# A two-block fp32 network on one core: SyncE stores queued one step behind the work that makes them, and FFN operands made one block in advance

## The chip, the cores and the metric

One core of a Trainium2 chip runs the whole network in one program. The metric is the device time of one execution in microseconds (us). Lower is better.

## What is computed

Block 1 puts four mixers side by side (mLSTM, SGU, a convolution, S5), joins them through `w_out`, and then runs the part that the change touches:

```python
x = layer_norm(ALPHA * x + g1 * y, ln1_w[l], ln1_b[l])
x = layer_norm(ALPHA * x + g2 * swiglu(x * (1.0 + sc2) + sh2, w_ffn_in[l], w_ffn_out[l]), ln2_w[l], ln2_b[l])
# swiglu: g, u = split(h @ w_in); (silu(g) * u) @ w_out
```

x has 1024 tokens of 1024 features, and the hidden width is 2816; all of it is in fp32. Block 2 (retention, sparse attention, a gated embedding) follows and is left as it is.

## The kernel before

**Arithmetic.** Every large product is made of three fp32r products. `K.split` writes a high part on ScalarE (ACT, L173, or L176 with a scale) and the rest on VectorE (DVE, L174 or L177), and `K.gemm` issues three matmuls per pair (L184 to L186: high by high, high by low, low by high).

**FFN input.** The 2816 hidden columns go in 22 blocks j of 128 (gate and up together). Each block is a product of 2 by 2 blocks done with seven products instead of eight, of 12 matmuls of 128x512 each: `Ffn.one` (two gate products, operands "11" and "12"), `two` (s2 by t2, s1 by t1), `three` (s4 by 22, s3 by t3) and `four` (22 by t4), 84 matmuls per block. For the weights, `Ffn.load` fetches two raw pages of w_ffn_in (L409), GpSimd (POOL) makes four sums (fsa, fsb: L424, L425, L429, L430), and seven splits make the operands `fw`. The activations come from `low_half` (11, 21) and `high_half` (t1, t2, 22, t3, t4), once, in the head of this stage. `first` issues the gate products of blocks 0 and 1, and `rest` goes through the blocks with the gate products two blocks ahead.

**FFN output.** `stage_b` takes the hidden blocks in 8 groups of two or three. For each group, 8 token tiles of two halves each are multiplied (18 matmuls per tile where the group has three hidden blocks) and DVE adds the result into `acc` (L615). `load(blk)` brings the next group: activations from scratch memory through `wload` (L160), weights (L562) with a POOL product by g2 (L563), and splits of both.

**What else runs there.** `residual()` reads 8 tiles back (L542), scales them (DVE L543, POOL L544) and stores them (L545). `spare` is the generator `presplit`: it loads 28 tiles of block 2's w_in (L771) and 16 of two later weights (by `wload`), splits them and stores both parts (L777, L783). `Ffn.four` stores each hidden block to scratch (L484).

**What sets the order.** The generators are advanced by hand in `stage_b`; the tile framework then places each instruction on its engine's queue. All loads and stores stand in one queue, SyncE's (SP), and are issued in its order: an issue that waits holds all behind it. Fetched fp32 pages come from a ring of three raw pages (`rp`, NR = 3), everything else from 46 pages (`qp`). PSUM has two rings of four banks (`mm`, `ax`).

Of the kernel before, what the change touches and what calls it, by code (L numbers as in the profile page):

```python
# [21 lines left out]
DFF = 2816  # L22
# [94 lines left out]
class K:  # L117
    def __init__(self, tc, es):
        self.tc, self.nc = tc, tc.nc
        self.es = es  # L120
# [135 lines left out]
class Front:  # L256
# [101 lines left out]
    def high_half(self):  # L358

        k, nc, page, s1, t1, hf, B = self.k, self.k.nc, self.k.page, self.s1, self.t1, self.hf, self.B  # L360
        fs, sp = [], {}

        def split(n, i, x):
            if i % 2 == 0:
                sp[n] = [page(f"{n}{c}{i}", F32R, [128, 2, 512]) for c in "hl"]
            hi, lo = (x[:, i % 2] for x in sp[n])
            nc.scalar.activation(hi, x, AF.Copy)
            nc.vector.tensor_tensor(lo, x, hi, op=ALU.subtract)
            B[n].append((hi, lo))
# [19 lines left out]
        for i in range(4):  # L389
            yield 1  # L390
            nc.gpsimd.tensor_tensor(fs[i][:, 0], fs[i][:, 1], fs[i][:, 0], op=ALU.subtract)
            split('t3', i, fs[i][:, 0])
        hf.clear()


class Ffn:
# [1 line left out]


    def __init__(self, k, B, w_fi, act):  # L400
        self.k, self.B, self.w_fi, self.act, self.w, self.o, self.keep = k, B, w_fi, act, {}, {}, {}

    def load(self, j):

        k, nc = self.k, self.k.nc
        raw = []
        for i in range(2):
            r = k.raw([128, 8, 128])
            nc.sync.dma_start(r, dap(self.w_fi, (i * (DFF // 128) + j) * 131072, [[1024, 128], [128, 8], [1, 128]]))  # L409
            raw.append(r)  # L410
        (a11, a12), (a21, a22) = [(r[:, 0:4], r[:, 4:8]) for r in raw]
        self.w[j] = w = {}

        def split(n, x):
            p = k.wpage("fw", shape=[128, 2, 4, 128])
            k.split(p[:, 0], p[:, 1], x)
            w[n] = p[:, 0], p[:, 1]

        split('11', a11)
        split('12', a12)  # L420
        yield 1
# [4 lines left out]
        split('s1', sp[:, 0])  # L426
        split('s2', sp[:, 1])
        yield 1
        nc.gpsimd.tensor_tensor(sq[:, 0], a12, sp[:, 1], op=ALU.subtract)  # L429
        nc.gpsimd.tensor_tensor(sq[:, 1], a11, a21, op=ALU.subtract)  # L430
        split('s4', sq[:, 0])
        yield 1
        split('s3', sq[:, 1])
        split('22', a22)

    def prod(self, j, a, b, pool):
        k, nc = self.k, self.k.nc
        ps = pool.tile([128, 512], F32, name="mm" if pool is k.mm else "ax")
        a, B = self.w[j].pop(a), self.B[b]
# [14 lines left out]
    def two(self, j):  # L454

        k, nc = self.k, self.k.nc
        e, u = self.o[j] = self.o[j], k.page("fu", shape=[128, 2, 512])
        nc.vector.tensor_tensor(u[:, 0], self.prod(j, 's2', 't2', k.ax), e[:, 1], op=ALU.add)
        yield 1
        nc.vector.tensor_tensor(u[:, 1], self.prod(j, 's1', 't1', k.ax), u[:, 0], op=ALU.add)  # L460

    def three(self, j):

# [10 lines left out]
    def four(self, j):  # L474
# [10 lines left out]
        del self.w[j]  # L485

    def first(self):
        self.ld = [self.load(0), self.load(1), self.load(2)]
        next(self.ld[0])
        next(self.ld[1])  # L490
        yield 1
        while len(self.B['21']) < 4:
            yield 1
        for j in range(2):
            yield from self.one(j)
            yield 1
            for _ in self.ld[j]:
                pass

    def rest(self):  # L500
        n = DFF // 128
        ld = self.ld[2]
        for j in range(n):
            for _ in self.two(j):
                next(ld, None)
            yield j, 0
            if j:
                self.four(j - 1)
            next(ld, None)
            for _ in self.three(j):  # L510
                next(ld, None)
            for _ in ld:
                pass
            ld = self.load(j + 3) if j + 3 < n else iter(())
            next(ld, None)
            if j + 2 < n:
                for _ in self.one(j + 2):
                    pass
            yield j, 1
        self.four(n - 1)  # L520


KEPT = (19, 20, 21)
FBLOCKS = ((19, 20), (21, 0, 1), (2, 3, 4), (5, 6, 7), (8, 9, 10), (11, 12, 13), (14, 15, 16), (17, 18))

# [1 line left out]
def stage_b(k, front, mod_s, ln1_w, ln1_b, w_fo, ln2_w, ln2_b, x2_s, sink, early, pre_sink, after, background, spare):  # L527
# [5 lines left out]
    def residual():  # L533
# [6 lines left out]
        for t in range(8):  # L540
            r = page("resid")
            nc.sync.dma_start(r, dap(res, t * 131072, [[1024, 128], [1, 1024]]))  # L542
            nc.vector.tensor_tensor(r, r, aw, op=ALU.mult)  # L543
            nc.gpsimd.tensor_tensor(r, r, ab, op=ALU.add)  # L544
            nc.sync.dma_start(dap(res2, t * 131072, [[1024, 128], [1, 1024]]), r)  # L545
            yield 1

    def load(blk):

        A, W = [], []  # L550
        yield A, W
        for j in blk:
            if j in keep:
                e = keep.pop(j)
                hl = page("ah", F32R), page("al", F32R)
                k.split(*hl, e)
                A.append(hl)
            else:
                A.append(k.wload(dap(act, j * 131072, [[1024, 128], [1, 1024]]), [128, 1024]))
            yield 1  # L560
            raw = k.raw()
            nc.sync.dma_start(raw, dap(w_fo, j * 131072, [[1024, 128], [1, 1024]]))  # L562
            nc.gpsimd.tensor_tensor(raw, raw, g2[0], op=ALU.mult)  # L563
            hl = page("whi", F32R), page("wlo", F32R)
            k.split(*hl, raw)
            W.append(hl)
            yield 1

    rs = residual()
    ahead = load(FBLOCKS[0])  # L570
    for j, st in front.ffn.rest():
        if st == 0 and 2 <= j < 18:
            for _ in range(1 + j % 2):
                next(spare, None)
        if st == 1 and j >= 2:
# [4 lines left out]
        if (j, st) == (19, 1):  # L580
            for t in range(8):
                acc[t] = page(f"acc{t}")
                nc.sync.dma_start(acc[t], dap(res2, t * 131072, [[1024, 128], [1, 1024]]))
        if (j, st) == (21, 0):
            nxt = next(ahead)
            next(ahead)
            next(ahead)
    for n, blk in enumerate(FBLOCKS):
        last = n == len(FBLOCKS) - 1
        for _ in ahead:  # L590
# [2 lines left out]
        if n == 5:  # L593
            early()
        if last:
            for _ in spare:
                pass
# [35 lines left out]
        else:  # L633
            for t in range(8):
                for _ in next(items):
                    pass
                next(ahead, None)
                if t % 3 == 1:
                    next(spare, None)


# [61 lines left out]
class StageC:  # L703
# [61 lines left out]
    def presplit(self):  # L765

        k, nc, w = self.k, self.k.nc, self.I['w_in']
        for b, (c0, n) in enumerate(WBLOCKS):
            for kk in range(0, 8, 2):
                raw = k.raw([128, 2, n])  # L770
                nc.sync.dma_start(raw, dap(w, kk * 128 * 3512 + c0, [[3512, 128], [128 * 3512, 2], [1, n]]))  # L771
                hi = k.wpage("phi", shape=[128, 2, n])
# [3 lines left out]
                for i, x in enumerate((hi, lo)):  # L776
                    nc.sync.dma_start(self.wsplit_at(b, kk, i, n), x.rearrange("p a b -> p (a b)").bitcast(F32))  # L777
                yield None
        for m, (w, sc, n) in enumerate(self.late):
            for kk in range(8):  # L780
                hl = k.wload(dap(w, kk * 131072, [[1024, 128], [1, 1024]]), [128, 1024], sc[:, kk:kk + 1] if kk < n else None)
                for i, x in enumerate(hl):
                    nc.sync.dma_start(self.wlate_at(m, kk, i), x.bitcast(F32))  # L783
                yield None

    @property
# [1752 lines left out]
```

## Time and profile before

| | |
|---|---|
| median of 3 runs | 2141.87 us (2139.83 to 2141.97) |
| the profiled execution | 2143.97 us, span 2142.2 us |
| mean granted TensorE clock | 0.962 of full |
| PE busy | 1978.5 us, 92% |
| DVE, ACT, POOL busy | 67%, 40%, 26% |
| DMA | 157 GB/s over the span |

Times are read from the start of the span. The high half of the activations is made from 622 to 667 us, the FFN's input products run until about 1089, its output products until about 1342, and block 2 takes the rest. A wait "X <- Y" says that engine line X was idle until Y was done. A busy PE (TensorE) can still be slow: the granted clock says at which of its two levels it ran.

### The profile page before, as it was taken

The page shows a single profiled execution, that of the slowest core. Times are in us where ns is not written, and L with a number is a line of the kernel's source. Part 1 is how long each engine was busy: PE and PEld are TensorE (multiplying, and loading weights), DVE is VectorE, ACT ScalarE, POOL GpSimd, SP SyncE. Part 2 cuts the span into 40 slices and gives each one's busy share as a digit, 9 for nine tenths or more (in the row PEclk, how much of TensorE's full clock was granted, in tenths as well). Part 3 has the DMA queues.
Part 4 walks back from the last instruction along what each step waited for, and adds up shares of the span by engine and source line. Part 5 has one row for each costly group of instructions (what it writes and reads, how often), then busy time and mean ns, then how long its engine had stood idle before and what let it go on. Part 6 is the DMA issues. An engine that isn't in the chain of part 4 may idle for free. (4 is left out here: it accounts for less than half of the span.)

```text
span 2142.2 us, 29434 instructions
## 1 busy us (share of the span) xinstructions
PE 1978.5 (92%) x10544; PEld 1630.6 (76%) x10544; DVE 1426.6 (67%) x2832; ACT 848.7 (40%) x1696; POOL 558.2 (26%) x557
## 2 busy tenths in 40 slices
PE   8798898999987989999999889899999998899998
PEld 3797888877865877778887768786787786688886
DVE  6968636476788567767666584957788746856533
ACT  2521234342144333334323220545787625355432
POOL 1454403112144333432412210331011221200032
PEclk9999898989998999999999999999999998999999
DMA  8465464456612566655556764313412205343611
GB/s 290 157 161 145 137 196 149 166 174 213 221 49 68 174 214 235 228 209 205 213 176 237 253 235 162 138 40 105 151 50 89 88 26 162 129 153 119 226 60 69
DMA packets 154419, 336.05 MB, mean 157 GB/s; under 512 B 31768, under 2 KB 71192, under 8 KB 154272
## 3 DMA queue, kind: packets, MB, share of 16 engines
q1 hardware_dynamic: 154272, 334.16, 46.2%
q8 instruction: 83, 1.36, 0.3%
q14 instruction: 64, 0.52, 0.1%
HBM read 227.16 MB, written 105.91 MB: 155 GB/s over the span
## 5 line engine op out<-in xcount | busy, mean ns | idle before, releaser
L184 PE MATMUL mm<-whi,xTh 128*128 128x512 f32 (+1 forms) x576 | 229.0, 401 | 4.9 <-DMA whi<-scr_wsp 3.6
L185 PE MATMUL mm<-wlo,xTh 128*128 128x512 f32 (+1 forms) x576 | 226.1, 393 | 2.1 <-DMA wlo<-scr_wsp 2.1
L186 PE MATMUL mm<-whi,xTl 128*128 128x512 f32 (+1 forms) x576 | 224.9, 393 | 0.0
L184 PE MATMUL mm<-whi,hhi 128*128 128x256 f32 (+1 forms) x512 | 151.7, 296 | 1.6 <-ACT zd L1651 0.9
L186 PE MATMUL mm<-whi,hlo 128*128 128x256 f32 (+1 forms) x512 | 149.2, 292 | 1.9 <-POOL hlo L1553 1.5
L173 ACT ACTIVATE whi<-raw 128x1024 fp32r<-128x1024 f32 (+2 forms) x74 | 76.6, 1044 | 187.2 <-POOL raw L563 98.3
L185 PE MATMUL mm<-wlo,hhi 128*128 128x256 f32 (+1 forms) x512 | 150.0, 293 | 0.0
L174 DVE TENSOR_TENSOR wlo<-raw,whi 128x1024 fp32r<-128x1024 f32 (+2 forms) x74 | 95.0, 1284 | 75.9 <-ACT whi L173 75.8
L184 PE MATMUL ax<-whi 128*128 128x512 f32 x304 | 123.6, 406 | 17.4 <-DVE acc L615 17.3
L184 PEld LDWEIGHTS mm<-whi,xTh 128*128 128x128 f32 x576 | 109.5, 191 | 27.5 <-DMA whi<-scr_wsp 5.4
L185 PEld LDWEIGHTS mm<-wlo,xTh 128*128 128x128 f32 x576 | 109.9, 191 | 22.0 <-DMA wlo<-scr_wsp 2.9
L186 PEld LDWEIGHTS mm<-whi,xTl 128*128 128x128 f32 x576 | 109.8, 191 | 21.5 <-DVE xTl L849 0.8
L185 PE MATMUL ax<-wlo,whi 128*128 128x512 f32 x304 | 121.5, 400 | 0.7 <-DVE wlo L174 0.7
L186 PE MATMUL ax<-whi,wlo 128*128 128x512 f32 x304 | 121.3, 399 | 0.0
L952 ACT ACTIVATE junk<-score,candf 128x384 bf16<-128x384 f32 (+1 forms) x124 | 96.1, 775 | 34.2 <-DVE candf L973 31.6
L563 POOL TENSOR_TENSOR raw<-raw,g2b 128x1024 f32<-128x1024 f32 x22 | 55.9, 2542 | 196.3 <-DMA raw<-in_w_ffn_out 133.3
L184 PEld LDWEIGHTS mm<-whi,hhi 128*128 128x128 f32 x512 | 100.8, 197 | 3.8 <-ACT zd L1651 1.3
L186 PEld LDWEIGHTS mm<-whi,hlo 128*128 128x128 f32 x512 | 100.5, 197 | 3.2 <-POOL hlo L1553 1.9
L185 PEld LDWEIGHTS mm<-wlo,hhi 128*128 128x128 f32 x512 | 100.8, 197 | 0.8 <-issue 0.6
L615 DVE TENSOR_TENSOR acc<-ax,acc 128x512 f32<-128x512 f32 x128 | 84.3, 682 | 23.1 <-PE ax L186 23.1
L184 PEld LDWEIGHTS ax<-whi 128*128 128x128 f32 x304 | 59.0, 194 | 36.5 <-DVE acc L615 21.8
L184 PE MATMUL mm<-hh,fw 128*128 128x512 f32 x176 | 72.1, 410 | 14.6 <-ACT fw L173 14.6
(687 smaller groups left out, 5464.1 us busy)
## 6 DMA issues: line engine op xcount, KB each, us to landing
raw<-in_w_fi_o SPq DMA_DIRECT2D x44, 512.0 KB
wmr<-in_w_mod SPq DMA_DIRECT2D x32, 512.0 KB
raw<-in_w_in_2o SPq DMA_DIRECT2D x24, 512.0 KB
scr_wsp<-phi SPq DMA_DIRECT2D x24, 512.0 KB
scr_wsp<-plo SPq DMA_DIRECT2D x24, 512.0 KB
whi<-scr_wsp SPq DMA_DIRECT2D x24, 512.0 KB
wlo<-scr_wsp SPq DMA_DIRECT2D x24, 512.0 KB
raw<-in_w_ffn_out SPq DMA_DIRECT2D x22, 512.0 KB
```

Source lines behind the costliest of these rows:

```text
L173: nc.scalar.activation(hi, raw, AF.Copy)
L174: nc.vector.tensor_tensor(lo, raw, hi, op=ALU.subtract)
L184: nc.tensor.matmul(ps, ah, bh, start=k == 0, stop=False)
L185: nc.tensor.matmul(ps, ah, bl, start=False, stop=False)
L186: nc.tensor.matmul(ps, al, bh, start=False, stop=k == n - 1)
L563: nc.gpsimd.tensor_tensor(raw, raw, g2[0], op=ALU.mult)
L615: nc.vector.tensor_tensor(v[:, cs], ps, v[:, cs], op=ALU.add)
L952: nc.scalar.activation(junk[:, :w], x, AF.Sign, scale=-1.0, bias=c, accum_out=cnt[:, j:j + 1])
```

## The change

Stores: `put` remembers a store, `tick` issues what was remembered at the next step, behind that step's work. Splits of spare weights, residual tiles and FFN-out loads come one step after their load. `Ffn.load` is cut in three: `fetch` (the DMA), `gates` (two splits) and `sums` (POOL and five splits); `rest` makes gates and sums of block j+1 during block j, has four steps per block in place of two, and issues the gate products one block ahead, after the first three blocks' have been issued in `first`. The raw pages of the first blocks come from the 46 pages ("fr"). `high_half` makes t1 and t2, then 22, then t3, then t4 (before: t4 ahead of 22). `two` multiplies s1 by t1 first. Spare halves are advanced more often during FFN input (56 half steps, 28 items; before 24 items) and five halves per FFN-out group (before three whole items).

```diff
+    def put(self, *pairs):
+        self.puts += pairs
+    def tick(self):
+        for dst, src in self.puts:
+            self.nc.sync.dma_start(dst, src)
+        self.puts = []
...
         for i in range(4):
-            nc.gpsimd.tensor_tensor(hf[i + 4], hf[i + 4], hf[i], op=ALU.subtract)
-            split('t4', i, hf[i + 4])
-        for i in range(4):
             yield 1
             split('22', i, fs[i][:, 1])
...
+        for i in range(4):
+            nc.gpsimd.tensor_tensor(hf[i + 4], hf[i + 4], hf[i], op=ALU.subtract)
+        for i in range(4):
+            yield 1
+            split('t4', i, hf[i + 4])
...
-            nc.sync.dma_start(dap(self.act, j * 131072, [[1024, 128], [1, 1024]]), e)
+            k.put((dap(self.act, j * 131072, [[1024, 128], [1, 1024]]), e))
...
     def first(self):
+        for j in range(AHEAD):
+            self.fetch(j, 0, self.k.page)
+        self.fetch(0, 1, self.k.page)
         yield 1
+        self.gates(0)
+        self.gates(1)
         while len(self.B['21']) < 4:
             yield 1
+        sums = self.sums(0)
+        for j in range(AHEAD):
             yield from self.one(j)
+            if j + 2 < AHEAD:
+                self.gates(j + 2)
+            else:
+                next(sums, None)
+            yield 1
+        for _ in sums:
+            yield 1
+        self.fetch(1, 1, self.k.page)
+
+    def rest(self):
+        n = DFF // 128
+        for j in range(n):
+            nxt, new = j + 1 < n, AHEAD <= j + 1 < n
+            if new:
+                self.gates(j + 1)
+            sums = self.sums(j + 1) if nxt else iter(())
+            for _ in self.two(j):
                 pass
+            next(sums, None)
             yield j, 0
             if j:
                 self.four(j - 1)
+            next(sums, None)
+            yield j, 1
             for _ in self.three(j):
                 pass
+            next(sums, None)
+            yield j, 2
+            for i in range(2):
+                if j + 2 < n and (j + 2, i) not in self.raw:
+                    self.fetch(j + 2, i)
+            if new:
+                for _ in self.one(j + 1):
                     pass
+            yield j, 3
         self.four(n - 1)
...
+                raw = k.raw()
+                nc.sync.dma_start(raw, dap((act, w_fo)[m], j * 131072, [[1024, 128], [1, 1024]]))
+                if last is not None:
+                    done()
+                last = m, j, raw
+                yield 1
+        done()
...
     for j, st in front.ffn.rest():
+        k.tick()
+        if 2 <= j < 21 and (st < 2 or j % 2):
+            next(spare, None)
+        if 1 <= j < 19 and st in (0, 2):
+            next(rs, None)
...
+                k.tick()
                 next(ahead, None)
-                if t % 3 == 1:
+                if t % 3:
                     next(spare, None)
```

In the queues it moves the following. First POOL, in the head (hg and hf are the sources of t3 and t4, fsa and fsb the weight sums), before:

```order
L391 TENSOR_TENSOR hg_5886<-hg_5886 128x512
L384 TENSOR_TENSOR hf_5822<-hf_5822,hf_5737 128x512
L424 TENSOR_TENSOR fsa<-raw 128x512
L425 TENSOR_TENSOR fsa<-fsa,raw 128x512
L391 TENSOR_TENSOR hg_5924<-hg_5924 128x512
L429 TENSOR_TENSOR fsb<-raw,fsa 128x512
L430 TENSOR_TENSOR fsb<-raw 128x512
```

and after:

```order
L396 TENSOR_TENSOR hg_5886<-hg_5886 128x512
L401 TENSOR_TENSOR hf_5822<-hf_5822,hf_5737 128x512
L396 TENSOR_TENSOR hg_5930<-hg_5930 128x512
L396 TENSOR_TENSOR hg_5964<-hg_5964 128x512
L401 TENSOR_TENSOR hf_5822<-hf_5822,hf_5737 128x512
L401 TENSOR_TENSOR hf_5854<-hf_5854,hf_5776 128x512
L437 TENSOR_TENSOR fsa<-fr 128x512
L439 TENSOR_TENSOR fsb<-fr 128x512
L438 TENSOR_TENSOR fsa<-fsa,fr 128x512
L440 TENSOR_TENSOR fsb<-fr,fsa 128x512
```

Block 0's weight sums stood third on POOL and stand seventh.

SP in the middle of the input products, before (w_in_2o is a spare tile, phi and plo its parts, scr_act a hidden block, resid a residual tile):

```order
L771 DMA raw<-in_w_in_2o 128x2x512
L777 DMA scr_wsp<-phi 128x1024
L777 DMA scr_wsp<-plo 128x1024
L409 DMA raw<-in_w_fi_o 128x1024 x2
L771 DMA raw<-in_w_in_2o 128x2x512
L542 DMA resid<-scr_res 128x1024
L484 DMA scr_act<-fe 128x1024
```

and after:

```order
L137 DMA scr_wsp<-phi 128x1024
L137 DMA scr_act<-fe 128x1024
L137 DMA scr_wsp<-plo 128x1024
L571 DMA resid<-scr_res 128x1024
L419 DMA raw<-in_w_fi_o 128x1024
L811 DMA raw<-in_w_in_2o 128x2x512
L137 DMA scr_res_104<-resid 128x1024
```

Where a spare's two stores stood between its own load and the weight fetches, weight fetches now stand between the stores of an earlier spare and the next spare's load, one at a time.

SP in the output products, before (scr_wlp takes the late spare weights):

```order
L783 DMA scr_wlp<-wlo 128x1024
L160 DMA raw<-scr_act 128x1024
L783 DMA scr_wlp<-whi 128x1024
L783 DMA scr_wlp<-wlo 128x1024
L562 DMA raw<-in_w_ffn_out 128x1024
L160 DMA raw<-in_w_ple_gate 128x1024
```

and after:

```order
L599 DMA raw<-scr_act 128x1024
L599 DMA raw<-in_w_ffn_out 128x1024
L137 DMA scr_wlp<-phi 128x1024
L599 DMA raw<-scr_act 128x1024
L137 DMA scr_wlp<-plo 128x1024
L822 DMA raw<-in_w_ple_gate 128x1024
```

The stores of a spare tile stood ahead of the next weight load; now a hidden block's and a weight's load go ahead of them.

## Rows read from the trace of the kernel before

**Rows 1.** Page, part 1: PE's busy time and share, instructions.
```profile
PE 1978.5 (92%) x10544; PEld 1630.6 (76%) x10544; DVE 1426.6 (67%) x2832; ACT 848.7 (40%) x1696; POOL 558.2 (26%) x557
```

**Rows 2.** Windows of the head: stretch, length, PE, PEld, DVE, ACT, POOL busy (count), clock, DMA share, GB/s.
```profile
622.00:667.00 45.00, 27.23 (x95) 19.32 (x93) 43.00 (x41) 27.62 (x47) 30.34 (x20) 0.74 0.18 56
...
680.00:740.00 60.00, 60.00 (x266) 49.70 (x265) 34.06 (x51) 18.52 (x32) 18.27 (x12) 1.00 0.44 147
```

**Rows 3.** Waits of PE from 622 to 680: total us, times, longest.
```profile
PE ax L184 <- ACT hg L378: 6.3, 1, 6.3
PE ax L184 <- ACT 22h L367: 5.0, 1, 5.0
PE ax L184 <- ACT t2h L367: 2.2, 1, 2.2
```

**Rows 4.** Groups of DVE instructions from 622 to 680: count, busy us, mean ns, idle before.
```profile
L174 DVE TENSOR_TENSOR fw<-fsa,fw 128x512 fp32r<-128x512 f32 x6 | 8.1, 1360 | 0.1
...
L174 DVE TENSOR_TENSOR fw<-raw,fw 128x512 fp32r<-128x512 f32 x7 | 5.0, 749 | 0.0
...
L368 DVE TENSOR_TENSOR t4l<-hf,t4h 128x512 fp32r<-128x512 f32 x4 | 4.9, 1220 | 0.0
```

**Rows 5.** Windows of the input products, columns as in rows 2.
```profile
780.00:820.00 40.00, 33.18 (x134) 26.79 (x133) 32.60 (x40) 15.48 (x26) 14.54 (x8) 0.87 0.62 224
820.00:860.00 40.00, 38.10 (x161) 30.81 (x160) 30.02 (x37) 15.39 (x26) 16.48 (x10) 0.96 0.64 230
860.00:900.00 40.00, 37.27 (x164) 30.23 (x163) 29.40 (x39) 14.96 (x26) 16.45 (x10) 1.00 0.67 243
900.00:940.00 40.00, 36.90 (x155) 29.73 (x154) 30.34 (x42) 15.51 (x27) 12.58 (x9) 0.96 0.60 210
```

**Rows 6.** Waits of PE and of SP's queue from 680 to 1089.
```profile
PE mm L184 <- ACT fw L173: 14.6, 4, 6.8
...
SPq L777 <- ACT phi L176: 114.8, 20, 9.8
SPq L484 <- DVE fe L479: 93.6, 13, 13.2
```

**Rows 7.** Timeline of SP's queue, 745 to 790: start, us, line, out<-in.
```profile
752.12 3.92 SPq L409 DMA_DIRECT2D raw<-in_w_fi_o  x2
...
775.75 0.38 SPq L771 DMA_DIRECT2D raw<-in_w_in_2o  x1
782.86 0.32 SPq L777 DMA_DIRECT2D scr_wsp<-phi  x1
...
784.11 1.63 SPq L409 DMA_DIRECT2D raw<-in_w_fi_o  x2
```

**Rows 8.** Windows of the output products, columns as in rows 2.
```profile
1140.00:1190.00 50.00, 45.05 (x186) 35.28 (x184) 26.13 (x32) 13.62 (x13) 13.35 (x5) 0.97 0.72 251
1190.00:1240.00 50.00, 43.50 (x180) 34.55 (x180) 29.73 (x36) 15.51 (x16) 12.83 (x5) 0.97 0.71 240
1240.00:1290.00 50.00, 44.87 (x179) 35.54 (x180) 39.71 (x50) 15.28 (x16) 9.70 (x4) 0.93 0.67 233
```

**Rows 9.** Waits of PE, DVE and SP's queue from 1089 to 1342.
```profile
PE ax L184 <- DVE acc L615: 18.0, 13, 2.3
...
DVE wlo L174 <- ACT whi L173: 67.1, 23, 4.9
...
SPq L783 <- ACT whi L176: 30.2, 9, 5.9
```

**Rows 10.** Timeline of SP's queue, 1140 to 1165.
```profile
1146.18 0.45 SPq L160 DMA_DIRECT2D raw<-scr_act  x1
1146.68 0.76 SPq L562 DMA_DIRECT2D raw<-in_w_ffn_out  x1
```

**Rows 11.** Timeline of DVE, same stretch; in brackets the wait before and its releaser.
```profile
1153.08 1.22 DVE L174 TENSOR_TENSOR wlo<-raw,whi 128x1024 fp32r<-128x1024 f32 x1 [4.90 <-ACT whi L173]
...
1157.69 1.23 DVE L174 TENSOR_TENSOR wlo<-raw,whi 128x1024 fp32r<-128x1024 f32 x1 [2.78 <-ACT whi L173]
```

More of the change, by code (lines that the diff above doesn't have):

```diff
@@ L389, in high_half @@
         for i in range(4):
+            nc.gpsimd.tensor_tensor(fs[i][:, 0], fs[i][:, 1], fs[i][:, 0], op=ALU.subtract)
+        for i in range(4):
             yield 1
-            nc.gpsimd.tensor_tensor(fs[i][:, 0], fs[i][:, 1], fs[i][:, 0], op=ALU.subtract)
             split('t3', i, fs[i][:, 0])
+        for i in range(4):
+            nc.gpsimd.tensor_tensor(hf[i + 4], hf[i + 4], hf[i], op=ALU.subtract)
+        for i in range(4):
+            yield 1
+            split('t4', i, hf[i + 4])
         hf.clear()
@@ L400, in __init__, with fetch, split, gates @@
     def __init__(self, k, B, w_fi, act):
-        self.k, self.B, self.w_fi, self.act, self.w, self.o, self.keep = k, B, w_fi, act, {}, {}, {}
-    def load(self, j):
-        k, nc = self.k, self.k.nc
[L406 to L421, printed above, removed]
+        self.k, self.B, self.w_fi, self.act, self.w, self.o, self.keep, self.raw = k, B, w_fi, act, {}, {}, {}, {}
+    def fetch(self, j, i, page=None):
+        nc = self.k.nc
+        r = self.raw[j, i] = (page or self.k.raw)(*(() if page is None else ("fr",)), shape=[128, 8, 128])
+        nc.sync.dma_start(r, dap(self.w_fi, (i * (DFF // 128) + j) * 131072, [[1024, 128], [128, 8], [1, 128]]))
+    def split(self, j, n, x):
+        p = self.k.wpage("fw", shape=[128, 2, 4, 128])
+        self.k.split(p[:, 0], p[:, 1], x)
+        self.w[j, n] = p[:, 0], p[:, 1]
+    def gates(self, j):
+        r = self.raw[j, 0]
+        self.split(j, '11', r[:, 0:4])
+        self.split(j, '12', r[:, 4:8])
+    def sums(self, j):
+        k, nc = self.k, self.k.nc
+        (a11, a12), (a21, a22) = [(r[:, 0:4], r[:, 4:8]) for r in (self.raw.pop((j, 0)), self.raw.pop((j, 1)))]
         sp = k.page("fsa", shape=[128, 2, 4, 128])
@@ L425, in load @@
         nc.gpsimd.tensor_tensor(sp[:, 1], sp[:, 0], a11, op=ALU.subtract)
-        split('s1', sp[:, 0])
-        split('s2', sp[:, 1])
+        nc.gpsimd.tensor_tensor(sq[:, 1], a11, a21, op=ALU.subtract)
+        nc.gpsimd.tensor_tensor(sq[:, 0], a12, sp[:, 1], op=ALU.subtract)
+        self.split(j, 's1', sp[:, 0])
+        self.split(j, 's2', sp[:, 1])
         yield 1
-        nc.gpsimd.tensor_tensor(sq[:, 0], a12, sp[:, 1], op=ALU.subtract)
-        nc.gpsimd.tensor_tensor(sq[:, 1], a11, a21, op=ALU.subtract)
-        split('s4', sq[:, 0])
+        self.split(j, 's3', sq[:, 1])
+        self.split(j, '22', a22)
         yield 1
-        split('s3', sq[:, 1])
-        split('22', a22)
+        self.split(j, 's4', sq[:, 0])
     def prod(self, j, a, b, pool):
@@ L508, in rest @@
                 self.four(j - 1)
-            next(ld, None)
+            next(sums, None)
+            yield j, 1
             for _ in self.three(j):
-                next(ld, None)
-            for _ in ld:
-                pass
[L514 to L517, printed above, removed]
+                pass
+            next(sums, None)
[5 more added lines that the diff above has]
+                for _ in self.one(j + 1):
                     pass
-            yield j, 1
+            yield j, 3
         self.four(n - 1)
+AHEAD = 3
 KEPT = (19, 20, 21)
@@ L542, in residual, with done @@
             nc.sync.dma_start(r, dap(res, t * 131072, [[1024, 128], [1, 1024]]))
+            yield 1
             nc.vector.tensor_tensor(r, r, aw, op=ALU.mult)
             nc.gpsimd.tensor_tensor(r, r, ab, op=ALU.add)
-            nc.sync.dma_start(dap(res2, t * 131072, [[1024, 128], [1, 1024]]), r)
+            k.put((dap(res2, t * 131072, [[1024, 128], [1, 1024]]), r))
             yield 1
     def load(blk):
-        A, W = [], []
+        A, W, last = [], [], None
+        def done():
+            m, j, raw = last
+            if m:
+                nc.gpsimd.tensor_tensor(raw, raw, g2[0], op=ALU.mult)
+            hl = (page("whi", F32R), page("wlo", F32R)) if m else (page("ah", F32R), page("al", F32R))
+            k.split(*hl, raw)
+            (W if m else A).append(hl)
         yield A, W
         for j in blk:
[L553 to L567, printed above, removed]
+            for m in range(2):
+                if j in keep and not m:
+                    hl = page("ah", F32R), page("al", F32R)
+                    k.split(*hl, keep.pop(j))
+                    A.append(hl)
+                    continue
+                raw = k.raw()
[3 more added lines that the diff above has]
+                last = m, j, raw
+                yield 1
+        done()
     rs = residual()
@@ L571, in stage_b @@
     for j, st in front.ffn.rest():
[L572 to L575, printed above, removed]
+        k.tick()
+        if 2 <= j < 21 and (st < 2 or j % 2):
+            next(spare, None)
+        if 1 <= j < 19 and st in (0, 2):
             next(rs, None)
@@ L579, in stage_b @@
             k.bcast(g2[0], mod_s, 5120, 1024)
-        if (j, st) == (19, 1):
-            for t in range(8):
+        if (j, st) == (20, 3):
+            nxt = next(ahead)
+        if (j, st) in ((20, 3), (21, 1), (21, 2)):
+            next(ahead, None)
+        if j == 21 and st < 2:
+            for t in range(st * 4, st * 4 + 4):
                 acc[t] = page(f"acc{t}")
                 nc.sync.dma_start(acc[t], dap(res2, t * 131072, [[1024, 128], [1, 1024]]))
[L584 to L587, printed above, removed]
     for n, blk in enumerate(FBLOCKS):
@@ L595, in stage_b @@
         if last:
+            k.tick()
             for _ in spare:
-                pass
+                k.tick()
+            k.tick()
             w2c = k.col('ln2_w'), k.col('ln2_b')
@@ L780, in presplit @@
             for kk in range(8):
-                hl = k.wload(dap(w, kk * 131072, [[1024, 128], [1, 1024]]), [128, 1024], sc[:, kk:kk + 1] if kk < n else None)
-                for i, x in enumerate(hl):
-                    nc.sync.dma_start(self.wlate_at(m, kk, i), x.bitcast(F32))
+                raw = k.raw()
+                nc.sync.dma_start(raw, dap(w, kk * 131072, [[1024, 128], [1, 1024]]))
+                yield None
+                hl = k.wpage("phi"), k.wpage("plo")
+                k.split(*hl, raw, sc[:, kk:kk + 1] if kk < n else None)
+                k.put(*((self.wlate_at(m, kk, i), x.bitcast(F32)) for i, x in enumerate(hl)))
                 yield None
```

23 lines of the change are left out of this document (8 added, 15 removed).

## The prediction

> **What bounds the kernel now.** I read the page first: TensorE is busy for 92% of the span [rows 1], so the time is the sum of its matmuls and of the holes between them, and a change that alters no matmul count can only close holes. The change reaches from the head of the FFN (622 us) to the end of its output products (1342 us). I read this stretch by windows, then asked for each hole what ended it, then read the queue of the engine that was late. Block 2 behind 1342 us is not touched, and its work stands on the same engine in the same order, so what is saved before it stays saved.
>
> The yardstick is the clean stretch from 680 to 740 us: 266 matmuls in 60.00 us, 0.2256 us each, at the full clock [rows 2]. A window that holds fewer matmuls than 4.43 per us has lost the difference, whether by idling or by the half clock that follows a hole (0.87 granted in the worst window [rows 5]). Records that are missing make this a little too large. Three places lose time:
>
> - The head, 622 to 667 us: 95 matmuls instead of 199.5, 23.6 us lost, at a granted clock of 0.74 [rows 2]. Some of these are transposes, so this is an upper figure. What is seen as waits is 6.3 + 5.0 + 2.2 = 13.5 us, all for pieces of the high half that ACT had not made [rows 3].
> - The input products, 780 to 940 us: 134 + 161 + 164 + 155 = 614 matmuls instead of 709, 95 missing, 21.5 us [rows 5]. Only four waits make it, 14.6 us, all for a gate operand `fw` [rows 6]; the rest is the clock.
> - The output products, 1140 to 1290 us: 186 + 180 + 179 = 545 instead of 665, 120 missing, 27 us [rows 8]. The waits are many and short: 13 for DVE's `acc`, 18.0 us [rows 9].
>
> Together at most 72 us can be had.
>
> **The change, part by part.**
>
> *Stores one step behind their makers.* No transfer goes away. What changes is what stands behind a waiting store on SP's queue. In the input products SP waited 114.8 us for phi and 93.6 us for the hidden block [rows 6], and the queue shows what that does: the spare's load goes at 775.75, its store at 782.86, after a whole load, split and wait, and only then, at 784.11, the next two pages of w_ffn_in [rows 7]. The fetches before had gone at 752.12, 32 us earlier, while a block of 84 matmuls lasts 84 x 0.2256 = 18.9 us. So the gate operand was late by some 7 us, which is the longest wait of 6.8 us [rows 6]. In the new order of SP a weight fetch has no store ahead of it whose maker isn't a step old.
>
> *Operands one block ahead.* This adds no instruction: seven splits and four sums per block as before. It gives 18.9 us of slack between the moment an operand is made and the moment it is read, more than the longest wait seen, 6.8 us. I expect the four waits to go and their half clock with them: 21.5 less about 2.5 for one short wait left, **19 us**. Bounds: 21.5 if all goes, 8 if the two longest fetch delays remain because the raw ring is still three pages and residual and spares now run through it until j = 20 (6.8 + about 7 of the 21.5 left over). The cover of the four more spare items in this stage (28, not 24) is DVE's idle time: 4 items of two phi and plo splits, about 4 x 2 x 0.75 = 6 us of DVE (the price of a split that stands beside nothing [rows 4]) in a stage where it is busy some 30 of 40 us [rows 5].
>
> *The head.* Three things move. Block 2's gate products, 24 matmuls or 24 x 0.2256 = 5.4 us, come forward into the hole; they are then missing later, where TensorE runs full, so up to 5.4 us is gained. The four t4 splits (4.9 us of DVE [rows 4]) go behind 22 and t3, which can shorten the 5.0 us wait for 22h. Against this, DVE gets two gate splits and one addition earlier (3 x 0.75 = 2.2 us), ACT as much, and on POOL block 0's sums stand behind six subtractions instead of two. I take 5.4 + about half of 5.0 less 2.2, **6 us**; bounds 0 (the hole only moves behind the sums of block 0) and 13.5 (all waits gone).
>
> What speaks about the head is how VectorE's time depends on POOL: a split of the same size takes 1360 ns from fsa, while POOL is at work, and 749 ns from raw [rows 4], and VectorE is busy 43.0 of 45 us there [rows 2]. The Trainium skill (SBUF — State Buffer, Who interferes with whom) says that a VectorE instruction with two inputs in SBUF and a GpSimd instruction that reads SBUF take one port pair in turn, each for its whole length. By that rule a reordering of VectorE and POOL work shortens nothing, and the head's gain would be 0 and the sum 32 instead of 38; the rows here show the stretch, not whether it is a lock. I keep 6 us, since the hole is filled with TensorE work that waits for neither.
>
> *The output products.* Here DVE stands 67.1 us, 23 times, in front of a split whose high part ACT has not made, with `acc` behind it in the same queue [rows 9], and TensorE waits for `acc` when its four banks are full. The split is late because its page is late: a weight load issued at 1146.68 was split at 1157.69, 11.0 us later, a hidden block's issued at 1146.18 at 1153.08, 6.9 us later [rows 10, 11]. The loads in turn stood behind stores that waited 30.2 us for a late spare's high part alone [rows 9]. The stores now go behind the loads, the ring serves about 57 pages in this stage instead of 61 (four spare items went forward), and splits are asked for one tile, 18 x 0.2256 = 4.06 us, later, against a mean DVE wait of 67.1 / 23 = 2.9 us. The ring of three pages stays, and by its own count it is near its limit: 222 us of matmuls / 57 x 3 = 11.7 us per page, against 11.0 + 1.2 for a weight and 6.9 + 1.2 for a hidden block. So I expect half of the loss to go: **13 us**; bounds 0 and 27, and on the other side the rival below.
>
> *Nothing for the rest:* `two` in the other order and the fr pages cost no instruction.
>
> **Sum.** 6 + 19 + 13 = 38 us off the profiled execution's 2143.97 us is 2106 us; the median of the runs shown is 2.1 us below that execution, so I forecast **2104 us**.
>
> **Rivals.**
>
> 1. *The stores leave, the ring stays the bound* (not all is done that the change says). Loads still wait for pages; the output products gain nothing and the input products keep half: 0 to 4 of the head, 10, 0 to 4: about 14 us, 2128 us. For it: three pages and the near-limit count above. Against it: in the stretch of rows 7 the fetch waits for a store, not for a page.
>
> 2. *VectorE and POOL are the bound of the input products.* VectorE 30.3 and POOL 15.0 of 40 us on average in rows 5 add up to 45 of 40; if they had to take turns, no order would help that stage. Gain: head 0, input 0, output 13: 2129 us. This is what the port rule of the Trainium skill (SBUF — State Buffer, Who interferes with whom) would give. Against it: VectorE's times already contain such waiting, and from 680 to 740 us TensorE ran full with both at work.
>
> 3. *The other side: pages held one tile longer.* In the output products a page is now given back a tile later, because its split is. If SP cannot run ahead, a page is taken for (12.2 + 8.1) / 2 + 4.06 = 14.2 us, and 57 pages through a ring of three take 57 / 3 x 14.2 = 270 us, 17 us more than the 253 us of the stage now; this decides as soon as a page's time exceeds 253 / 19 = 13.3 us. With nothing gained in the head and only 8 in the input products the sum is 2141.87 + 17 - 8 = 2151 us. For it: the page count. Against it: SP's queue no longer stands before stores, so the next load is issued as soon as a page is free, and both pages of a pair may wait side by side.
>
> 4. *All three holes close:* 13.5 + 21.5 + 27 = 62 us, 2080 us.
>
> **How the numbers follow.** Forecast case (2092 to 2118 us) 0.50, rivals 1 and 2 together (2120 to 2134 us) 0.23, rival 4 (below 2092 us) 0.11, no change because gains and losses cancel 0.07, rival 3 (slower) 0.09. What a measurement of this kernel can tell from no change is about 0.2%, 4.3 us. So faster 0.84, same 0.07, slower 0.09. The range, for 8 in 10, runs from 2084 us (most of rival 4's case) to 2136 us (beyond rivals 1 and 2).
>
> **What would show it.** Right: in the windows of the input products 177 matmuls per 40 us throughout, no wait for `fw`, SP's waits for phi and the hidden block near 0; in the output products fewer and shorter waits for `acc`, DVE's waits for whi well below 67 us; in the head block 2's gate products before the first s1 product, and a shorter wait for 22h. Wrong: SP's waits come back at the raw pages (its loads waiting for a split), waits for fsa on ACT with TensorE idle behind them in the head, or more waits for `acc` than 13. A stretch in block 2 that differs by more than 2 us would break the assumption that nothing changes there.

## The result and the profile after

The changed kernel takes **2103.06 us** (median of 4 runs, 2101.67 to 2106.3) against 2141.43 us for the kernel before: ratio **0.9824 [0.9807, 0.9841]**, 38.4 us less. The forecast was 2104 us.

The page of the changed kernel, part 1 and the clock's line of part 2; as many matmuls as in [rows 1]:

```profile
PE 1960.9 (93%) x10544; PEld 1616.6 (77%) x10544; DVE 1424.3 (68%) x2832; ACT 846.3 (40%) x1696; POOL 558.1 (27%) x557
...
PEclk9999899989998999999999999999999998999999
```

To see where the time went I use four marks: on TensorE the last transpose of the high half, and on VectorE the first and the last addition of 22 by t4 and the last `acc` of the seventh output group. For the kernel before and the changed one the two additions read:

```profile
682.26 0.69 DVE L478 TENSOR_TENSOR fu<-mm,fu 128x512 f32<-128x512 f32 x1 [1.30 <-PE mm L186]
...
1088.33 0.69 DVE L478 TENSOR_TENSOR fu<-mm,fu 128x512 f32<-128x512 f32 x1 [0.80 <-PE mm L186]
```

```profile
670.47 0.67 DVE L492 TENSOR_TENSOR fu<-mm,fu 128x512 f32<-128x512 f32 x1
...
1054.52 0.69 DVE L492 TENSOR_TENSOR fu<-mm,fu 128x512 f32<-128x512 f32 x1 [0.68 <-PE mm L195]
```

| us | head | stage I (input products) | stage O (output, 7 groups) | all behind |
|---|---|---|---|---|
| before | 50.7 | 406.1 | 248.3 | 805.6 |
| changed | 43.4 | 384.1 | 241.3 | 804.7 |
| gain | 7.3 | 22.0 | 7.0 | 0.9 |

In both kernels TensorE goes from the last product 22 by t4 straight into the output products (at 1088.12 and 1054.32 us), so the last addition is a fair end of stage I. The remaining 4.4 us of the two profiled executions lie ahead of the head (last transpose at 631.5 and 627.1 us). Nothing shows them to be the change's: the kernel before and three variants of it that are alike up to there came to this mark between 622 and 632 us.

Windows of the changed kernel, columns as in [rows 2]; they answer to [rows 2], [rows 5] and [rows 8], some 30 us earlier:

```profile
622.00:667.00 45.00, 32.62 (x118) 22.07 (x117) 39.69 (x43) 23.57 (x41) 28.43 (x19) 0.89 0.04 12
...
780.00:820.00 40.00, 39.21 (x172) 31.80 (x171) 30.98 (x40) 15.48 (x26) 16.33 (x10) 1.00 0.71 251
820.00:860.00 40.00, 40.00 (x178) 33.14 (x177) 30.68 (x43) 16.30 (x28) 16.03 (x11) 1.00 0.65 230
...
1150.00:1200.00 50.00, 43.35 (x187) 34.32 (x186) 29.60 (x38) 13.69 (x13) 12.77 (x5) 1.00 0.72 248
1200.00:1250.00 50.00, 44.06 (x186) 34.93 (x185) 37.06 (x48) 15.53 (x16) 13.09 (x5) 0.98 0.74 251
```

The input products run full at the full clock from 820 us on (178 matmuls in 40 us) and nearly so in the window before (172), where there were 134 to 164. The head is better but not closed. The output products are nearly as bad as before: 187 and 186 matmuls in 50 us, against 186, 180 and 179. The waits of TensorE in the three stretches (622 to 680, 680 to 1070, 1054 to 1296 us) say the same:

```profile
PE ax L193 <- ACT fw L182: 6.1, 1, 6.1
PE ax L194 <- DVE t3l L377: 2.2, 3, 0.7
```

```profile
PE mm L195 <- DVE fw L183: 1.6, 2, 0.8
```

```profile
PE ax L193 <- DVE acc L654: 16.1, 10, 3.5
```

The wait for 22h [rows 3] is gone, the one for hg has been replaced by one of the same size for block 0's first sum operand, the waits for `fw` fell from 14.6 to 1.6 us, and those for `acc` only from 18.0 to 16.1.

SP's waits for phi fell from 114.8 to 41.4 us, but it waits more than before for raw pages that POOL's sums still read (680 to 1070 us). The prediction had named waits at the raw pages as a sign of being wrong; here TensorE runs full all the same:

```profile
SPq L811 <- POOL fsb L440: 50.6, 9, 7.6
...
SPq L137 <- ACT phi L185: 41.4, 28, 4.7
...
SPq L419 <- POOL fsb L440: 30.9, 9, 5.2
```

### The profile page after: what moved, and what is told of

Its sections match the earlier page's. It is cut to its first block, busy times and chain, and to the rows that moved or that the text cites. A ratio compares the mean times of both kernels' runs of the same rounds, so it can differ in the third digit from the quotient of the medians.

```text
span 2100.5 us, 29426 instructions
## 1 busy us (share of the span) xinstructions
PE 1960.9 (93%) x10544; PEld 1616.6 (77%) x10544; DVE 1424.3 (68%) x2832; ACT 846.3 (40%) x1696; POOL 558.1 (27%) x557
## 5 line engine op out<-in xcount | busy, mean ns | idle before, releaser
L193 PE MATMUL ax<-whi,ah 128*128 128x512 f32 x352 | 140.6, 400 | 16.6 <-DVE acc L654 16.5
L194 PE MATMUL ax<-wlo,ah 128*128 128x512 f32 x352 | 139.1, 395 | 0.4 <-DVE wlo L183 0.4
L195 PE MATMUL ax<-whi,al 128*128 128x512 f32 x352 | 138.7, 394 | 0.0
L195 PEld LDWEIGHTS mm<-whi,xTl 128*128 128x128 f32 x576 | 108.6, 189 | 21.1 <-DVE xTl L892 0.8
L182 ACT ACTIVATE whi<-raw 128x1024 fp32r<-128x1024 f32 (+2 forms) x51 | 52.9, 1040 | 140.0 <-POOL raw L585 98.9
L183 DVE TENSOR_TENSOR wlo<-raw,whi 128x1024 fp32r<-128x1024 f32 (+2 forms) x51 | 65.0, 1277 | 61.3 <-ACT whi L182 61.1
L193 PEld LDWEIGHTS ax<-whi,ah 128*128 128x128 f32 x352 | 67.1, 191 | 36.2 <-DVE acc L654 18.8
L798 POOL TENSOR_TENSOR rA<-rA 128x256 f32<-128x256 f32 x32 | 23.7, 740 | 229.9 <-DVE rA L797 164.8
```

What stands on the lines that cost most here:

```text
L182: nc.scalar.activation(hi, raw, AF.Copy)
L183: nc.vector.tensor_tensor(lo, raw, hi, op=ALU.subtract)
L193: nc.tensor.matmul(ps, ah, bh, start=k == 0, stop=False)
L194: nc.tensor.matmul(ps, ah, bl, start=False, stop=False)
L195: nc.tensor.matmul(ps, al, bh, start=False, stop=k == n - 1)
L798: eng2.tensor_tensor(ov, a, b, op=ALU.add)
```

## The experiments

The kernel before was timed anew beside each group of experiments, so ratios are compared, not times. Stages are from the one profile of each. The times of experiments quoted below are medians.

| | edit | ratio [95%] | head | I | O |
|---|---|---|---|---|---|
| before | | 1 | 50.7 | 406.1 | 248.3 |
| changed | | 0.9824 [0.9807, 0.9841] | 43.4 | 384.1 | 241.3 |
| e1 | changed, stores at makers | 0.9837 [0.9797, 0.9876] | 43.4 | 384.6 | 240.2 |
| e2 | changed, operands late | 0.9825 [0.9794, 0.9857] | 42.8 | 387.8 | 236.6 |
| e3 | before, stores put back | 1.0054 [1.0033, 1.0075] | 52.3 | 414.6 | 248.5 |
| e4 | changed, two blocks lead | 0.9845 [0.9817, 0.9872] | 38.6 | 385.2 | 237.5 |
| e5 | changed, splits with loads | 0.9890 [0.9870, 0.9910] | 43.4 | 394.4 | 240.2 |
| e6 | changed, fetch late | 0.9835 [0.9813, 0.9857] | 43.4 | 388.2 | 240.5 |
| e7 | before, fetch early | 0.9989 [0.9972, 1.0007] | 50.6 | 401.8 | 246.5 |
| e8 | changed, old high half | 0.9821 [0.9800, 0.9843] | 45.0 | 382.6 | 238.4 |
| e9 | before, spares spread | 0.9959 [0.9942, 0.9976] | 51.1 | 398.3 | 246.5 |
| e10 | changed, block 1's sums in the head | 0.9830 [0.9800, 0.9859] | 43.3 | 383.7 | 240.8 |
| e11 | changed, ten more spares in I | 0.9844 [0.9809, 0.9879] | 43.4 | 389.0 | 237.1 |
| e12 | changed, four raw pages | 0.9813 [0.9788, 0.9838] | 43.4 | 381.4 | 231.4 |

**e1, stores at their makers.**

```diff
     def put(self, *pairs):
-        self.puts += pairs
+        for dst, src in pairs:
+            self.nc.sync.dma_start(dst, src)
```

> The changed kernel with one thing undone: every store is issued right behind the work that makes it. I call stage I the time from the first to the last addition of the product 22 by t4 (before 406.1 us, changed 384.1 us). Theory 1, the stores in front of the loads in SP's queue made the stalls: stage I comes back to 398 to 406 us with waits of TensorE for fw of 8 us or more, and the time is about 2118 to 2126 us. Theory 2, operands made one block ahead give the slack whatever stands in the queue: stage I stays below 388 us, and the time within 5 us of 2103.

Stage I is 384.6 us, but that says nothing of theory 1. The instruction order shows why. On ACT, VectorE, POOL and TensorE the program is the same as the changed kernel's, and on SP a single store of one spare part differs by one place:

```
 DMA scr_act<-fe 128x1024
-DMA scr_wsp<-plo 128x1024
 DMA g2b<-scr_mod 128x1024
+DMA scr_wsp<-plo 128x1024
 DMA raw<-in_w_fi_o 128x1024
```

With the rest of the change in place, the framework puts the stores where `put` and `tick` put them. So the two methods add nothing to the changed kernel, and this run is a repetition of it: what the order of stores and loads on SP is worth stays open here.

It and e6, whose order is the changed kernel's too, tell how well a stage repeats: stage I is 384.1, 384.6 and 388.2 us. Stage O has one order on every engine in the changed kernel, e1, e2, e4, e6, e8 and e10, and lies between 236.6 and 241.3 us. So a difference of 4 us in stage I or 5 us in stage O between two profiles shows nothing; the head, alike in e1, e5, e6 and e11, is 43.4 us in each.

**e2, operands just ahead of their use.**

```diff
-            if new:
-                self.gates(j + 1)
-            sums = self.sums(j + 1) if nxt else iter(())
             for _ in self.two(j):
                 pass
...
+            if new:
+                self.gates(j + 1)
+            for _ in self.sums(j + 1) if nxt else ():
+                pass
             for i in range(2):
```

> The changed kernel with its stores as they are, but gates and sums of block j+1 made at the end of block j, just ahead of their use, and the next fetches behind them. Theory 1 (stores): stage I stays below 390 us, the time within 6 us of 2103. Theory 2 (operands one block ahead): stage I rises to 400 us or more, with waits for fw, and the time to 2118 us or more.

Stage I is 3.7 us longer, which is within the spread of the repetitions. Nor is it a test of theory 2: in the placed order the gate operands of blocks 3 to 21 are split 1.5 to 10.8 us ahead of their products, in the changed kernel 0.7 to 15.6 us, so the smallest lead became larger.

**e3, the kernel before with put and tick alone.** Its stores go through `put`, with a `tick` at each step, as in the diff of the change.

> The kernel before with one part of the change alone: its stores go through put and tick, all else as it was. Theory 1: stage I falls from 406 to about 388 us and the time to about 2122 us. Theory 2: stage I stays above 400 us, the time within 6 us of 2141.

Neither: 0.54% slower, and stage I 8.5 us longer. The placed order moved less than the edit: at its longest wait, and at the three others, the weight fetch now goes ahead of one store of a spare but still stands right behind the other, which waited for ACT:

```profile
775.93 0.32 SPq L134 DMA_DIRECT2D scr_wsp<-phi  x1
776.30 1.26 SPq L418 DMA_DIRECT2D raw<-in_w_fi_o  x2
```

So `put` and `tick` alone gain nothing. What a fetch ahead of both stores would gain was not run, and why the kernel became slower is not shown.

**e4, two blocks lead.** `AHEAD = 2`.

> The changed kernel with the gate products of two blocks ahead of the others instead of three. If the head's gain of about 12 us comes from block 2's 24 matmuls put into its hole, the head grows by about 5 us and the time is about 2108 us; if it comes from the order in which the high half is made, the head stays and the time is within 2 us of 2103.

The head of 38.6 us misleads: in e4 the wait for hg (7.12 us) stands ahead of the last transpose, so it has left the head. A mark ahead of all this is the last tile of the layer norm in front of the FFN; for the kernel before, the changed one and e4 it reads as follows, with e4's first addition behind it:

```profile
620.03 0.81 DVE L320 TENSOR_SCALAR acc<-acc,rs_r,ln_nm 128x1024 f32<-128x1024 f32 x1
```

```profile
616.21 0.81 DVE L329 TENSOR_SCALAR acc<-acc,rs_r,ln_nm 128x1024 f32<-128x1024 f32 x1
```

```profile
614.22 0.81 DVE L329 TENSOR_SCALAR acc<-acc,rs_r,ln_nm 128x1024 f32<-128x1024 f32 x1
...
668.39 0.67 DVE L492 TENSOR_TENSOR fu<-mm,fu 128x512 f32<-128x512 f32 x1
```

From there to the first addition it takes 62.2 us before, 54.3 in the changed kernel and 54.2 in e4, which has block 2's 24 matmuls (5.4 us) behind this stretch and not in it. So in the changed kernel they cost the head nothing, as I had said. Yet the ratio doesn't separate from the change's, and stage I, which must then do them, is 1.1 us longer and not 5.4. Inconclusive for the total.

**What made `fw` late in the kernel before.** With both theories short, I read ACT's timeline there, ahead of TensorE's longest wait, and beside it the first spare's store on SP and the wait itself:

```profile
771.60 1.32 ACT L176 ACTIVATE phi<-raw,cols 128x512 fp32r<-128x512 f32 x2
781.50 1.34 ACT L176 ACTIVATE phi<-raw,cols 128x512 fp32r<-128x512 f32 x2 [8.58 <-DMA raw<-in_w_in_2o]
782.74 1.13 ACT L173 ACTIVATE fw<-fsb 128x512 fp32r<-128x512 f32 x2
783.78 0.61 ACT L173 ACTIVATE fw<-raw 128x512 fp32r<-128x512 f32 x1
789.00 1.15 ACT L173 ACTIVATE fw<-raw 128x512 fp32r<-128x512 f32 x2 [4.60 <-DMA raw<-in_w_fi_o]
```

```profile
775.33 0.32 SPq L777 DMA_DIRECT2D scr_wsp<-plo  x1
```

```profile
789.68 0.79 PE L184 MATMUL mm<-hh,fw 128*128 128x512 f32 x1 [6.82 <-ACT fw L173]
```

The second spare of that step was loaded at 775.75, right behind the first one's store [rows 7]. ACT stood 8.58 us in front of its split, with three weight splits queued behind. Its stores went at 782.86 and 783.70, and behind them, at 784.11, the fetch of the two weight pages; ACT waited 4.60 us for it, and TensorE 6.82 us for the gate operand made of it. The three splits behind the spare aren't what TensorE waited for: that was the fetch. It stood behind a store of a spare, as the prediction had read it, and the three shorter waits end in the same way. In the whole of stage I the waits of ACT for transfers were these, before:

```profile
ACT fw L173 <- DMA raw<-in_w_fi_o: 56.2, 14, 5.9
ACT phi L176 <- DMA raw<-in_w_in_2o: 52.1, 8, 8.6
```

and after:

```profile
ACT fw L182 <- DMA raw<-in_w_fi_o: 14.1, 3, 5.1
```

ACT's wait for spares is gone. That gave theories 3 to 5.

**e5, splits in the step of their load.** In `presplit`, `residual` and `load(blk)` the yield between load and split is taken out and the generators advanced half as often (28 and 16 items as in the change).

> The changed kernel, but spare weights, residual tiles and output-product loads are split in the step that loads them; stores still one step behind, w_ffn_in fetched and made one block ahead as in the change. Neither the stores' place nor the operands' place had moved the time alone. Theory 3, the distance between a spare's or residual's load and its split keeps ACT and DVE from standing before a transfer: stage I (changed 384 us, before 406) rises to 396 us or more and the time by 10 us or more. Theory 4, it is the distance between the w_ffn_in fetch and its splits: stage I stays below 388 us.

The ratio rises to 0.9890, 14 us of the change's 38 are given back in the median, 10.3 us of them in stage I. That is more than the repetitions differ by, so the edit costs about what theory 3 had said. Its path is not the one that I had in mind: ACT's waits for spares don't come back, and TensorE waits for VectorE's part of operand 22 (680 to 1089 us):

```profile
PE ax L195 <- DVE fw L183: 8.6, 4, 3.1
```

```profile
ACT phi L185 <- DMA raw<-in_w_in_2o: 2.4, 1, 2.4
```

Stage O did not move (240.2): its loads were split with their load in this run too, so that part of the change gave nothing that can be seen.

**e6, fetch in the step of the split**, and **e7, the kernel before with one yield behind its fetch.**

```diff
+            for i in range(2):
+                if nxt and (j + 1, i) not in self.raw:
+                    self.fetch(j + 1, i)
             if new:
                 self.gates(j + 1)
```

```diff
         self.w[j] = w = {}
+        if j > 2:
+            yield 1
```

> The changed kernel, but the two pages of w_ffn_in of block j+1 are fetched at the start of block j, in the step that splits them, instead of half a block to a block earlier. Theory 3: stage I stays below 388 us. Theory 4: ACT and DVE stand before the transfer, stage I rises to 396 us or more and the time to about 2115 us.

> The kernel before with one yield more in its load: the w_ffn_in pages are fetched at the end of block j and split at the start of block j+1, nothing else. Theory 4: stage I falls from 406 to about 390 us, the time to about 2125. Theory 3: stage I stays above 400 us and the time within 6 us of before.

Neither tests theory 4. In e6 the order of the instructions is the changed kernel's on every engine, SP's too, so its 4.1 us are a repetition's. In e7 the fetches at TensorE's four waits still went right behind a spare's stores, 6.0 to 6.3 us ahead of the products that need them (before 5.6 to 6.1); its 4.3 us are about what stage I differs by in repetitions, and its ratio doesn't separate from 1.

**e9, the kernel before with its spares spread.**

```diff
-        if st == 0 and 2 <= j < 18:
-            for _ in range(1 + j % 2):
-                next(spare, None)
+        if 2 <= j < 18 and (st == 0 or j % 2):
+            next(spare, None)
```

> The kernel before with one line changed: of the 24 spare items of the input products, the blocks with two now take one in each half instead of both in the first half. The split beside the load had explained about 10 of stage I's 22 us and the distance of fetch and operands about 4. Theory 5, the bunching of two items is most of what is left: stage I falls from 406 to 396 to 400 us, the time by 5 to 10 us. Rival: it stays above 403 us.

398.3 us: one line, without any other part of the change, takes 7.8 us out of stage I and is faster as a whole, 0.9959 [0.9942, 0.9976]. The waits for `fw` are 9.4 us instead of 14.6:

```profile
PE mm L184 <- ACT fw L173: 9.4, 3, 3.5
```

**What the profiles say together.** Two readings go across the runs. The first is the lead of a weight fetch: from its issue to the first gate product of its block. At the waits it was 5.6 to 6.1 us before, 6.0 to 6.3 in e3 and e7, 5.2 to 5.4 in e9. In the changed kernel it is never below 7.6 (7.1 in its repetition e1). In e5 it is down to 6.1 to 6.3 for three blocks. In e2 it is never below 17.5; there ACT waits for spares and SP for their split nearly as long as before (52.1 and 114.8 us), and TensorE hardly waits (680 to 1089 us):

```profile
ACT phi L185 <- DMA raw<-in_w_in_2o: 44.2, 13, 6.5
```

```profile
SPq L137 <- ACT phi L185: 111.8, 24, 7.6
```

```profile
PE mm L195 <- DVE fw L183: 4.0, 3, 1.6
```

So neither of these two waits costs the stage by itself; what goes with TensorE's loss in the kernel before and its variants is a fetch that comes late. No run changes that lead alone.

The second is where the waits lie. In every profile that has waits of TensorE in stage I, the last of them comes no more than 22 us, about one block, behind the last of the eight residual tiles. From 940 to 1060 us the kernel before runs full, with two spares in every second block until 1017 us:

```profile
980.00:1020.00 40.00, 40.00 (x178) 33.14 (x177) 28.02 (x41) 15.73 (x27) 13.31 (x9) 1.00 0.59 215
```

So two spares at once made TensorE wait only where residual tiles ran beside them. No run moves the residual tiles alone, so what they add is open.

**e8 and e10, the head.** e8 puts the old order back into `high_half`; e10 makes the sums of block 1 in `first`, behind those of block 0.

> The changed kernel with the old order in the high half: t4 is made ahead of 22 and t3. If this order gave the head its gain (from the last transpose to the first addition of 22 by t4: before 50.7 us, changed 43.4 us), the head grows by about 5 us and the wait for 22h returns; if not, the head stays within 2 us of 43.4.

> The changed kernel, but the weight sums and the five further splits of block 1 are made in the head, behind those of block 0, as they were before the change. If the head gained because these splits no longer stand on ACT and VectorE ahead of the activations' own, the head (43.4 us, before 50.7) grows by 4 to 7 us and a wait for 22 or t3 of some 5 us comes back. If not, it stays below 45 us.

e8 gives back 1.6 us and its total is that of the change; e10 gives back nothing. Both are weak tests: the framework places the splits, and against the changed kernel only 12 and 10 lines of difference stand on ACT, in 1696 instructions.

**e11 and e12, the output products.** e11 advances the spares in each of the four steps of blocks 2 to 20, and in two of eight tiles; e12 sets NR = 4 and NQ = 45.

> The changed kernel with ten more of the 44 spare items in the input products (one half in each of the four steps of blocks 2 to 20) and two half items per output group instead of five. I call stage O the time from the last addition of 22 by t4 to the last acc of the seventh group (before 248.3 us, changed 241.3). Theory 6, stage O gained because four items left it, some 2 us each: ten more bring it to about 225 us, stage I grows by less than 6 us, and the time is about 2092 us. Rival, the ring of three pages and not the spare work is the bound there: stage O stays above 236 us and the time is 2103 us or more.

> The changed kernel with four raw pages instead of three and 45 other pages instead of 46. Theory 7, the output products wait because a weight page is held through its load, the POOL product and both parts of its split, and the ring of three gives the next load no page: stage O (241.3 us) falls to 230 us or less, the waits for acc (16.1 us) to under 8 us, and the time to about 2090 us. Rival, the chain of load, POOL product and split is late for another reason (its place on the engines): stage O stays above 236 us and the time within 5 us of 2103.

Theory 6 falls: with ten spare items less, stage O is 237.1 us and not 225, no lower than with the same output code as the changed kernel's (236.6 to 241.3). With a fourth page it is 231.4 us, 9.9 less than the changed kernel's and 5.2 less than the lowest of those; the 2.7 us in stage I are within its spread. VectorE and SP show what the ring did, first the changed kernel (1054 to 1296 us), then e12 (1052 to 1284 us):

```profile
DVE wlo L183 <- ACT whi L182: 53.8, 16, 5.7
...
SPq L599 <- DVE wlo L183: 61.5, 15, 6.3
```

```profile
PE ax L193 <- DVE acc L654: 8.9, 9, 1.8
...
DVE wlo L183 <- ACT whi L182: 22.6, 7, 4.8
...
SPq L599 <- DVE wlo L183: 16.1, 4, 6.7
```

SP's wait for a page to be split fell from 61.5 to 16.1 us, and `acc`'s waits from 16.1 to 8.9. Theory 7 holds in mechanism, though stage O and the waits missed their marks by 1.4 and 0.9 us. The profiled execution is the shortest of all, a span of 2087.4 us, but the ratio, 0.9813 [0.9788, 0.9838], doesn't separate e12 from the change: their intervals overlap, and the kernel before was some 6 us faster beside e12 than beside the others. Whether e12 beats the change is left open.

## Why the prediction was right, and where it was not

**The sum.** Its terms were 6, 19 and 13 us; the marks give 7.3, 22.0 and 7.0. The head and the output products lie within their bounds, the input products half a microsecond above theirs of 21.5. That the total came within 1 us of the forecast is in part luck: one term was 3 us too small, another 6 too large.

**Input products: the size was nearly right, the parts were not.** The size came from a clean stretch in the same stage, and so did not depend on the cause. Of the cause, the reading of the queue holds: at the long waits a weight fetch stood behind a spare's store. (The working has a slip there: 32 us between two fetches less 18.9 is 13, not 7; 7.1 us is the time from the spare's load to its store.) Two steps failed. "Stores one step behind their makers" was to take the store away from ahead of the fetch; `put` and `tick` do nothing in the changed kernel (e1), and alone they leave a store ahead of the fetch and make the kernel slower (e3). "It gives 18.9 us of slack" did not come: from ACT's split to the first matmul with it, the first sum operand has 3.3 to 17.2 us in the changed kernel (blocks 1 to 21), where it had 21.1 to 32.4, and gate operands still come down to 0.7 us, as here:

```profile
762.69 1.15 ACT L182 ACTIVATE fw<-raw 128x512 fp32r<-128x512 f32 x2 [4.92 <-DMA raw<-in_w_fi_o]
```

```profile
763.39 0.48 PE L193 MATMUL mm<-hh,fw 128*128 128x512 f32 x1
```

What the runs put in its place are two sizes and a reading. Splitting spares, residual tiles and output loads a step later is worth about 10 us of stage I (e5), not asking for two spares at once about 8 (e9, on the kernel before). They were measured from different sides and needn't add up. The reading, which no run isolates, is that the fetch goes out earlier ahead of its product, at least 7.1 us where it had been down to 5.6. Which part of the change brings that, and what the residual tiles have to do with it, stays open.

**Head.** Block 2's gate products take no time in it (e4), as said. The other half of the term, t4 behind 22, was put at half of 5.0 us and is 1.6 us in e8. Together that is 7.0 us, about what the head gained: 7.3 us, or 8.0 counted from the layer norm. As feared in "block 0's sums stand behind six subtractions instead of two", a wait of 6.1 us for the first sum operand came up in place of the 6.3 for hg. The clock was 0.74 in the window from 622 to 667 us and is 0.89. By the rule of the Trainium skill on the shared port (SBUF — State Buffer, Who interferes with whom), that a VectorE instruction with two inputs in SBUF and a GpSimd instruction that reads SBUF take turns, reordering their work would have gained nothing. The 7.3 us do not decide that: most of them are TensorE work put into a hole, and no run here takes the two engines apart.

**Output products.** Over-sized: 7.0 for 13. The forecast named the three-page ring as near its limit; a fourth page takes 9.9 us off the changed kernel's stage (e12), so the ring still held it. Splits a tile later bought nothing that can be seen there (e5), nor did `put` and `tick` alone (248.5 in e3). Which part of the change gave the 7.0 is not settled.

**Rivals.** Rival 1 had the ring right for the output products. Rival 2 is refuted: stage I runs full with VectorE at 30.7 and POOL at 16.0 of 40 us. Rival 3 didn't come: pages held a tile longer cost stage O nothing that can be seen.

## What to carry to other kernels

Follow a wait of TensorE back to its transfer, and measure how long before its use that transfer was issued: other engines and queues may stand for long without a cost (e2). Ask for a load in one step and for the work on it in the next (e5), and spread pairs of loads evenly instead of two at a time (e9). And look at the placed order before crediting a reordering in the source: with a scheduling framework an edit may move nothing (e1, e6), or less than it says (e2, e3, e7).

## What the runs showed that I had not expected

Putting stores later in the kernel before made it slower, 1.0054 [1.0033, 1.0075], with stage I at 414.6 us. The change that was to make operands a block ahead left the sum operands less lead than they had. And kernels with the same code up to the last transpose reach it between 622 and 632 us, while a stage of 384 us with one and the same order of instructions came out at 384.1, 384.6 and 388.2 us: a gain of a few microseconds in one profile is no gain yet.
